# The order of copies and products in VectorE's queue, in a batched trace of matrix products

## The chip, the cores and the metric

One core of a Trainium2 chip. The metric is the device time of a run in microseconds (us), median of several runs. The profile's span, from the first to the last instruction, is about 1.7 us shorter.

## The reference

```python
def setup_inputs():
    B, N = 8, 2176
    return {
        "a": np.random.randn(B, N, N).astype(np.float32),
        "b": np.random.randn(B, N, N).astype(np.float32),
    }

def reference(a, b):
    prod = np.matmul(a, b)
    traces = np.diagonal(prod, axis1=1, axis2=2).sum(axis=-1)
    return traces.astype(np.float32)
```

The trace of a product is the sum over all i, k of a[i, k] * b[k, i]. So no matrix product is needed: transpose A, multiply elementwise by B, add up. Every input byte is read once.

## The kernel before

For each of eight batches: A is loaded as bf16 (the load casts) in two loads of 8 row tiles (4352 KB each) and one of a single row tile (544 KB). TensorE transposes A into PSUM tiles, of which there are five. ScalarE copies two of three of them to SBUF, VectorE the third. Then B is loaded in the same sizes and VectorE multiplies it by the transposed A, row tile by row tile, with a running sum. The large loads of A and B share three buffers, the single tiles two, and there is one buffer for the transposed A (`at`). In the last batch TensorE takes part of the products.

```python
    at_pool = ctx.enter_context(tc.tile_pool(name="at_pool", bufs=1))
    stage = ctx.enter_context(tc.tile_pool(name="stage", bufs=3))
    single = ctx.enter_context(tc.tile_pool(name="single", bufs=2))
    ...
    psum_pool = ctx.enter_context(tc.tile_pool(name="psum", bufs=5, space=bass.MemoryType.PSUM))
    # ... (cut)
    def evacuate(dst, src):
        nonlocal evacs
        if evacs % 3 == 2:
            nc.vector.tensor_copy(out=dst, in_=src)
        else:
            nc.scalar.copy(out=dst, in_=src)
        evacs += 1
    # ... (cut)
    for bi in range(BATCH):
        # ... loads of A; transpose_group() transposes and evacuates each group (cut)
        def on_dve(x, y):
            nonlocal cols
            multiply_reduce(x, y, acc[:, cols:cols + 1])
            cols += 1

        for start, m, count in joined(b_groups):
            # ... the last tile of the last batch (cut)
            groups, _ = load(b[bi], start, m, count)
            for start, m, b_t in groups:
                v0 = start // P
                for s in range(m):
                    row = b_t[:, s, :]
                    # ... the last batch's share for TensorE (cut)
                    on_dve(wide_at(at, v0 + s, 0, n_wide), wide(row, 0, n_wide))
                if not last:
                    on_dve(at[:, v0:v0 + m, split:], b_t[:, 0:m, split:])
```

The program is written in data-flow form; a scheduler fixes each engine's queue when the kernel is built. The order it chose had put the first product of a batch ahead of three copies of the same batch's transposed A, in batches 2 to 8.

## Time and profile before

| | before |
|---|---|
| time, median of 3 runs | 711.24 us (711.16 to 711.25) |
| span of the profiled run | 709.5 us |
| read from HBM | 303.04 MB |
| busy: VectorE, TensorE, ScalarE | 58%, 29%, 28% |

The prediction below shows the page, the chain, the waits and the timeline. Two more views are wanted. The first is the list of groups (columns: line, engine, operation, out<-in, shapes, count, then busy us and mean ns of one, then idle time before them and what ended it). It gives VectorE's copies and their sizes:

```profile
L109 DVE COPY at<-ps 128x1024 bf16<-128x1024 bf16 x64 | 78.4, 1224 | 171.3 <-PE ps L154 171.3
L109 DVE COPY at<-ps 128x512 bf16<-128x512 bf16 x32 | 13.5, 422 | 5.1 <-PE ps L175 4.8
L109 DVE COPY at<-ps 128x128 bf16<-128x128 bf16 x7 | 1.5, 221 | 2.6 <-PE ps L175 2.6
```

The second is the list of loads (tile, issuing queue, count, KB each, median us from issue to landing). One large load needs some 20.6 us by itself (an estimate: its 4.456 MB at the mean 216 GB/s of the trace); what is above that is time spent behind other loads:

```profile
t<-in_a_dram POOLq DMA_DIRECT2D x16, 4352.0 KB, 43.9
t<-in_b_dram POOLq DMA_DIRECT2D x15, 4352.0 KB, 51.7
```

### The profile page before, as it was taken

Reading aid. Unit: us, or ns where it says so; the run is one execution under the profiler, and the core shown is the slowest. Engines: PE = TensorE matmul, PEld = TensorE weight load, DVE = VectorE, ACT = ScalarE, POOL = GpSimd, SP = SyncE. Lnnn points to the kernel's source line nnn. Section 1 sums busy time; section 2 is a strip of 40 time slices with the busy share of each in tenths; the row PEclk is TensorE's granted clock in tenths of the full one; section 3 lists DMA queues with packets and bytes.
Section 4 is the critical chain, followed back from the end, with each engine's and each line's share of the span. In section 5 each row is a group of like instructions: output and inputs, shape, how many; then the busy total and the mean of one; then the engine's idle time right before and its main releaser. Section 6 shows DMA issues by size and latency. Waiting matters only on the chain.

```text
span 709.5 us, 3709 instructions
## 1 busy us (share of the span) xinstructions
PE 205.6 (29%) x1406; PEld 192.3 (27%) x1406; DVE 408.9 (58%) x449; ACT 197.3 (28%) x210; POOL 34.7 (5%) x60
## 2 busy tenths in 40 slices
PE   1442006410055100651005600056000660005637
PEld 0432006410055100551005500056000660004636
DVE  0222996129962299523995249942499325993257
ACT  2443005430064200652006610066000660006600
POOL 1000000000010000100001000000000000000000
PEclk9977556775577655776557765577555775557768
DMA  9999999999999999999999999999999999999997
GB/s 220 220 219 217 208 220 220 218 213 211 222 220 217 212 216 218 220 217 214 214 219 220 216 213 216 219 219 216 212 217 220 218 216 212 218 218 215 219 209 140
DMA packets 11620, 152.32 MB, mean 215 GB/s; under 512 B 850, under 2 KB 1106, under 8 KB 3282
## 3 DMA queue, kind: packets, MB, share of 16 engines
q0 software_dynamic: 11456, 150.97, 100.0%
q1 hardware_dynamic: 146, 1.11, 0.5%
q8 instruction: 11, 0.18, 0.1%
q14 instruction: 7, 0.06, 0.0%
HBM read 303.04 MB, written 0.00 MB: 427 GB/s over the span
## 4 chain that ended last, share of the span: by engine, by line
DMA 55%; DVE 34%; issue 7%; another core or an unknown queue 1%; ACT 1%; PE 1%; POOL 0%; DVEq 0%; POOLq 0%
DMA t<-in_b_dram 42%; DVE scratch L121 33%; DMA t<-in_a_dram 12%; DVE at L109 1%; ACT at L111 1%; PE ps L154 0%; DVE acc L121 0%; DVEq L121 0%; POOL identity masks.py:199 0%; PE ps L175 0%; POOL identity masks.py:197 0%; PE total L294 0%; DVE late L121 0%; DVE result L298 0%
## 5 line engine op out<-in xcount | busy, mean ns | idle before, releaser
L121 DVE CUSTOM_DVE_ANT_1 scratch<-at,t 128x2048 bf16<-128x2048 bf16 (+1 forms) x156 | 310.5, 1990 | 112.9 <-DMA t<-in_b_dram 106.4
L111 ACT COPY at<-ps 128x1024 bf16<-128x1024 bf16 x208 | 194.9, 1046 | 485.4 <-PE ps L154 485.4
L154 PE MATMUL ps<-identity,t 128*128 128x128 f32 x1071 | 178.4, 333 | 496.8 <-DMA t<-in_a_dram 291.5
L154 PEld LDWEIGHTS ps<-identity,t 128*128 128x128 f32 x1071 | 164.8, 213 | 506.6 <-issue 283.9
L109 DVE COPY at<-ps 128x1024 bf16<-128x1024 bf16 (+2 forms) x104 | 92.8, 902 | 179.0 <-PE ps L154 171.3
L74 POOL DMA_DIRECT2D t<-in_a_dram x23 | 15.3, 668 | 365.6 <-DVE acc L121 224.6
L74 POOL DMA_DIRECT2D t<-in_b_dram x26 | 16.7, 642 | 288.6 <-PE ps L175 151.9
L175 PE MATMUL ps<-identity,t 128*128 128x128 bf16 x170 | 17.0, 224 | 2.3 <-DVE at L109 1.8
L279 PEld LDWEIGHTS <-at 128*128 128x128 bf16 x153 | 16.9, 117 | 2.2 <-issue 2.1
L279 PE MATMUL trace_ps<-t,at 128*128 128x128 bf16 x144 | 16.2, 288 | 1.4 <-DMA t<-in_b_dram 1.4
L175 PEld LDWEIGHTS <-t 128*128 128x128 bf16 x170 | 13.4, 102 | 4.6 <-issue 4.2
L121 DVE DVE_READ_ACCUMULATOR2_ANT acc<- 128x1 f32 x163 | 13.3, 82 | 0.0
L86 DVE CAST t<-words 128x1088 bf16<-128x1088 f32 x1 | 0.7, 727 | 4.9 <-DMA words<-in_a_dram 4.9
L121 DVE CUSTOM_DVE_ANT_0 scratch<-at,t 128x128 bf16<-128x128 bf16 x7 | 2.0, 291 | 0.2
L85 ACT CAST t<-words 128x1088 bf16<-128x1088 f32 x1 | 1.1, 1098 | 3.8 <-DMA words<-in_a_dram 3.8
L243 POOL DMA_DIRECT2D b_t<-in_b_dram x3 | 1.6, 537 | 7.4 <-PE trace_ps L279 7.4
L121 DVE CUSTOM_DVE_ANT_1 scratch<-at,b_t 128x256 bf16<-128x256 bf16 (+1 forms) x3 | 1.5, 510 | 0.1
L271 DVE TENSOR_REDUCE sums<-acc 128x1 f32<-128x22 f32 (+1 forms) x8 | 1.4, 175 | 0.3
L279 PE MATMUL trace_ps<-b_t,at 128*128 128x128 bf16 x9 | 1.4, 291 | 0.4 <-DMA b_t<-in_b_dram 0.4
L85 ACT ACT_TABLE_LOAD x1 | 1.3, 1283 | 0.7 <-PEq L317 0.7
L294 PE MATMUL total<-late,ones 128*1 128x1 f32 x8 | 0.8, 164 | 0.8 <-DVE late L121 0.8
L294 PEld LDWEIGHTS total<-late,ones 128*1 128x1 f32 x8 | 0.3, 80 | 1.2 <-DVE late L121 1.2
(14 smaller groups left out, 2.7 us busy)
## 6 DMA issues: line engine op xcount, KB each, us to landing
t<-in_a_dram POOLq DMA_DIRECT2D x16, 4352.0 KB, 43.9
t<-in_b_dram POOLq DMA_DIRECT2D x15, 4352.0 KB, 51.7
t<-in_b_dram POOLq DMA_DIRECT2D x9, 544.0 KB, 54.6
t<-in_a_dram POOLq DMA_DIRECT2D x7, 544.0 KB, 44.2
t<-in_b_dram POOLq DMA_DIRECT2D x1, 2176.0 KB, 43.6
words<-in_a_dram SPq DMA_DIRECT2D x1, 1088.0 KB, 5.0
t<-in_b_dram POOLq DMA_DIRECT2D x1, 1088.0 KB, 28.8
b_t<-in_b_dram POOLq DMA_DIRECT2D x1, 256.0 KB, 8.9
```

The lines of the kernel that those rows point to most:

```text
L74: issued = nc.gpsimd.dma_start(out=part, in_=rows)
L85: nc.scalar.copy(out=t[:, 0, :half], in_=plain[:, :half])
L86: nc.vector.tensor_copy(out=t[:, 0, half:], in_=plain[:, half:])
L109: nc.vector.tensor_copy(out=dst, in_=src)
L111: nc.scalar.copy(out=dst, in_=src)
L121: nc.vector.tensor_tensor_reduce(out=out, in0=x, in1=y, scale=1.0, scalar=0.0, op0=MUL, op1=ADD, accum_out=acc,)
L154: nc.tensor.transpose(ps[:, n * m + r, :], words[:, r, c0:c0 + step * (P - 1) + 1:step], tiles[f32],)
L175: last_transpose = nc.tensor.transpose(ps16[:, n, r, :], a_t[:, r, c0:c0 + P], tiles[bf16],)
L243: nc.gpsimd.dma_start(out=row[:, lo:hi], in_=b[bi, start:start + P, lo:hi])
L271: nc.vector.reduce_sum(out=tiles["sums"][:, bi:bi + 1], in_=acc[:, :cols], axis=mybir.AxisListType.X)
L279: nc.tensor.matmul(trace_ps, x, y, start=(n == 0), stop=(n == len(pe_work) - 1),)
L294: nc.tensor.matmul(total[:, BATCH - 1:BATCH], tiles["ones"], part, start=(n == 0), stop=(n == len(parts) - 1),)
```

## The change

Its intent is to keep VectorE from standing at a product whose B has not landed while copies with data ready, which TensorE needs done, stand behind it. An ordering edge, without a semaphore, goes from each product to the last VectorE copy of its batch.

```diff
     evacs = 0
+    last_copy = None
 
     def evacuate(dst, src):
-        nonlocal evacs
+        nonlocal evacs, last_copy
         if evacs % 3 == 2:
-            nc.vector.tensor_copy(out=dst, in_=src)
+            last_copy = nc.vector.tensor_copy(out=dst, in_=src)
         else:
             nc.scalar.copy(out=dst, in_=src)
         evacs += 1
@@
+
+        copies_end = last_copy
         acc = acc_pool.tile([P, 2 * NT], f32, tag="acc")
         cols = 0
 
         def on_dve(x, y):
             nonlocal cols
-            multiply_reduce(x, y, acc[:, cols:cols + 1])
+            with tc.issue_after(copies_end.ins):
+                multiply_reduce(x, y, acc[:, cols:cols + 1])
             cols += 1
```

## The prediction

> **What bounds the kernel now.** I read the page first (busy shares, the slices, the queues, the chain), then the chain in order of time, the waits, the timeline of one batch, and the windows of the last microseconds. From the page:
>
> ```profile
> span 709.5 us, 3709 instructions
> PE 205.6 (29%) x1406; PEld 192.3 (27%) x1406; DVE 408.9 (58%) x449; ACT 197.3 (28%) x210; POOL 34.7 (5%) x60
> ...
> DMA  9999999999999999999999999999999999999997
> GB/s 220 220 219 217 208 220 220 218 213 211 222 220 217 212 216 218 220 217 214 214 219 220 216 213 216 219 219 216 212 217 220 218 216 212 218 218 215 219 209 140
> ...
> HBM read 303.04 MB, written 0.00 MB: 427 GB/s over the span
> ...
> DMA 55%; DVE 34%; issue 7%; another core or an unknown queue 1%; ACT 1%; PE 1%; POOL 0%; DVEq 0%; POOLq 0%
> ```
>
> No compute engine is over 58%. The DMA row is 9 in every slice but the last, and the rate row is flat at 208 to 222 GB/s (counted as bf16, half of what is read), from the first slice to the last but one. So the transfers never pause. The last line, the shares of the chain, seems to say otherwise: a third of the end's path runs through VectorE. The chain in order of time shows why:
>
> ```profile
> 198.33 45.16 DMA t<-in_b_dram
> 243.54 0.08 issue
> 243.62 2.29 DVE scratch L121
> 245.92 1.47 DVE at L109 x2
> 247.39 2.20 DVE scratch L121
> 249.59 0.15 DVE at L109
> ...
> 285.81 45.08 DMA t<-in_b_dram
> ```
>
> This is one turn of a loop: B's first load lands (243.5), VectorE multiplies both large loads of B, which frees the buffer, the next batch's first B load is issued (285.81) and lands 45 us later. The period is 285.81 - 198.33 = 87.5 us, 42.3 of VectorE and 45.2 of transfer. But a large load is 4352 KB, and at the mean 216 GB/s it needs 4.456 MB / 0.216 = 20.6 us. The other 24.6 us of its 45.2 are the loads queued ahead of it. They are slack: if VectorE ends earlier, the load is issued earlier and queues longer. A batch moves 2 x 17 tiles of 544 KB, 18.9 MB, which at 216.5 GB/s is 87.5 us: exactly the period. The loop turns at the transfers' rate.
>
> The defect that the change aims at is in the waits and the timeline:
>
> ```profile
> DVE scratch L121 <- DMA t<-in_b_dram: 106.4, 10, 13.7
> PE ps L154 <- DVE at L109: 103.2, 17, 14.6
> ```
> ```profile
> 243.62 2.29 DVE L121 CUSTOM_DVE_ANT_1 scratch<-at,t 128x2048 bf16<-128x2048 bf16 x1 [13.63 <-DMA t<-in_b_dram]
> 245.84 0.08 DVE L121 DVE_READ_ACCUMULATOR2_ANT acc<- 128x1 f32 x1
> 245.84 1.55 DVE L109 COPY at<-ps 128x1024 bf16<-128x1024 bf16 x2
> 247.11 0.73 PEld L154 LDWEIGHTS ps<-identity,t 128*128 128x128 f32 x4 [14.80 <-DVE at L109]
> ```
>
> VectorE stands 13.6 us at a product whose B has not landed, with three copies queued behind it. TensorE can't go on, because those copies hold PSUM tiles (there are five), and waits 14.6 us for the first of them. Both waits occur once per batch in batches 2 to 8; 7 x 14 us is most of both totals above.
>
> **What the Trainium skill says.** "Perfetto Trace Analysis", section "Per-engine timelines": ACT, DVE and GPSIMD are strict FIFO. The trace agrees: copies whose PSUM data was ready did not pass the waiting product. "DMA: Bandwidth & Descriptors", sections "Specifications" and "Measured": the fabric ceiling of a core is 435 GB/s, 425 were measured for a 16 MB load. The trace agrees: 427 GB/s over the span, and 2 x 216.5 = 433 in steady state, within 1% of the ceiling. "Perfetto Trace Analysis", "Identifying Performance Opportunities": improve the most-contended engine. Here that is the DMA engines, which this change gives no less work.
>
> **The change part by part.** It adds no instruction and removes none. It puts an ordering edge from each product of a batch to that batch's last VectorE copy, so the queue order on VectorE alone changes.
>
> 1. Batch 1: its lone row tile of A comes first, and the last copy already stands at 57.71 us, before the first product at 68.74. Nothing moves.
>
> 2. Batches 2 to 8: three copies (1224, 422 and 221 ns by the groups' rows) go ahead of the first product. TensorE filled the banks until about 232.5 us in the batch shown; the five copies and transposes left (three on VectorE, two on ScalarE at 1047 ns) then end near 235. B lands at 243.5, so the copies lie in idle time, with about 8 us to spare.
>
> 3. After B lands, VectorE has 1.87 us of copies less; they overlapped a little. The stretch from first product to the end of the first large B load is 177.79 - 156.14 = 21.65 us in batch 2, with copies, and 89.05 - 68.74 = 20.31 in batch 1, without. So VectorE gains about 1.3 us per batch. (A wait for the second B load, which lands 20.6 us after the first, may eat part.) The two A loads released by the first half and the B load released by the second are issued 1 to 1.5 us earlier. On the path this is nothing: the shortest time to landing of a large load in steady state is 42 us (issue at 178.09, landing 220.3) for 20.6 us of own transfer, so 21 us are queued ahead. The backlog grows to 22 to 23.
>
> 4. The last batch: its lone row of A releases the buffer of the last but one B tile. Its transposes, now at 686.2 behind the blocked copies, should run near 673, so that load goes out near 673 in place of 687.0. TensorE's products of B, queued behind those transposes (first at 686.49), start when B lands, near 682. The last B tile, now issued at 694.9, waits for the buffer of the first B load: TensorE's 72 products at 111 ns would end near 690, VectorE's four at 2.33 us near 691.3; it goes out near 691.5, 3.4 us earlier.
>
> Does that move the end? Windows of the last stretch (columns: PE, PEld, DVE, ACT, POOL busy, clock, DMA share, GB/s):
>
> ```profile
> 694.00:695.00 1.00, 1.00 (x12) 1.00 (x11) 1.00 (x1) 0.00 (x0) 0.10 (x1) 1.00 1.02 213
> ...
> 699.00:700.00 1.00, 0.11 (x2) 0.11 (x2) 0.00 (x0) 0.00 (x0) 0.00 (x0) 1.00 1.05 210
> ...
> 703.00:704.00 1.00, 1.00 (x12) 1.00 (x10) 0.97 (x3) 0.00 (x0) 0.00 (x0) 0.50 0.56 101
> 704.00:705.00 1.00, 0.80 (x7) 0.56 (x6) 0.96 (x4) 0.00 (x0) 0.00 (x0) 0.50 0.14 24
> ```
>
> The DMA share stays near 1 until 703. The last pieces, issued at 694.9 with 7.7 us queued ahead of 1.2 us of own transfer, came at line rate. Issued at 691.5 they would land at the same time. The last VectorE stretch begins at 700.00, when the two-row load lands at 699.85 (issued at 671.04, when the transposes of A's second large load are done, which does not change), and it runs without a gap to the end at 707.5. Before it VectorE stood idle for 2.4 us; that becomes about 3 to 4. TensorE had 0.4 us of waits left there and keeps up.
>
> Sum: 0 per batch on the path, 0 at the end. 711.24 less a few tenths at most.
>
> **The rivals.** (a) VectorE's share of the chain is real, and each turn gets shorter: 7 x 1.3 = 9 us, 702 us (1.3% faster). For it: the chain. Against: the flat rate, and 21 us of backlog. (b) The wait changes its name: products wait for the last copy in place of B. It would cost if the copy came after B. Against: A's lone row is issued before B in the same queue, so lands some 20 us earlier, and about 8 us are spare; only if the new order also delayed A's loads would a few us per batch be lost, 715 to 725. (c) The tail reorders. One single-row product (1.27 us) may move into VectorE's idle stretch before 700, which would end about 0.9 us earlier (limited by the last piece, which came at about 705.2): 710.3. Or TensorE, idle longer before 700, is slower: 0 to 1 us more, 712. Its matmuls there took 0.11 us at clock 0.5 as at 1.0, which speaks against it.
>
> **Range and chances.** I predict 711.1 us. 709.8 to 712.4 should hold it 8 times in 10: it covers (c) on both sides and a chip's own scatter. Faster by over 2% means under 697.0 us. The reads alone need 303.04 MB / 435 GB/s = 696.6 us by the skill's ceiling (an estimate), and start and tail add about 7: 0.01. Slower by over 2% (725.5) needs (b) at its worst: 0.02. Within 2%: 0.97.
>
> **What would show it right or wrong.** Right: the waits of TensorE for VectorE's copies fall from 103 us to a few; every large load's time to landing grows by 1 to 2 us; the rate row stays as it is; VectorE's busy time is unchanged and its wait for B stays near 100 us; the last B tile is issued near 691.5 but lands at about the same time. Wrong: slices of the rate row that rise by over 1% (then the DMA did have gaps), a period other than 87.5 us, products that wait for copies after B has landed, or large loads issued in another order.

## The result and the profile after

| | before | after |
|---|---|---|
| time, median of 6 runs each | 711.25 us (711.16 to 711.62) | 711.14 us (710.94 to 711.24) |
| span of the profiled run | 709.5 us | 709.4 us |

The ratio is 0.9997, 95% interval 0.9984 to 1.001. A ratio here is the mean time of one kernel's fast runs over the mean of the other's fast runs of the same rounds, so it is not quite the ratio of the medians in the table. The time is the same.

From the page of the kernel after, the rates of the 40 slices (share of the DMA engines, and GB/s counted as bf16):

```profile
DMA  9999999999999999999999999999999999999996
GB/s 220 220 220 219 206 219 220 219 217 209 219 220 218 217 212 216 220 219 215 212 218 220 218 213 215 215 222 217 215 214 213 225 217 212 215 217 222 219 207 138
```

The transfers look as before. In the trace's records of single packets there is no moment without one in flight between 1.8 us and the last data, at 704.9 us before and 704.8 after.

The waits of the kernel after (who, for whom, us in total, times, longest; its line numbers are one higher than before):

```profile
DVE at L110 <- PE ps L155: 196.9, 64, 19.9
DVE scratch L122 <- DMA t<-in_b_dram: 67.7, 17, 10.4
PE ps L155 <- DVE at L110: 2.7, 8, 0.4
```

TensorE's wait for VectorE's copies fell from 103.2 us to 2.7. The change does what it was made for. But TensorE's idle time before transposes, whatever it is put down to, fell only from 496.8 to 482.5 us: by the profile's account most of that wait has been traded for waits for the next batch's A and for the end of a batch's products. VectorE's wait for B fell from 106.4 to 67.7 us and its wait for TensorE grew by 26 us: the same idle time, cut differently, because copies now lie in the middle of it. The timeline of the third batch shows them there:

```profile
231.22 1.22 DVE L110 COPY at<-ps 128x1024 bf16<-128x1024 bf16 x1 [0.83 <-PE ps L155]
...
232.92 0.42 DVE L110 COPY at<-ps 128x512 bf16<-128x512 bf16 x1 [0.47 <-PE ps L176]
233.18 0.70 POOL L74 DMA_DIRECT2D t<-in_a_dram  x1 [20.62 <-PE ps L176]
...
234.24 0.22 DVE L110 COPY at<-ps 128x128 bf16<-128x128 bf16 x1 [0.89 <-PE ps L176]
234.50 0.56 POOL L74 DMA_DIRECT2D t<-in_a_dram  x1 [0.63 <-PE ps L176]
243.52 2.29 DVE L122 CUSTOM_DVE_ANT_1 scratch<-at,t 128x2048 bf16<-128x2048 bf16 x1 [9.05 <-DMA t<-in_b_dram]
```

The three copies end at 234.46, and VectorE is idle for 9.05 us until B lands. The two lines of POOL show a thing that the prediction did not foresee: from the fourth batch on, A's single tile (the shorter issue at 234.50) is now issued ahead of A's second large load. Before, it came behind it. The transposes that release its buffer now end earlier; that the scheduler moved it for this reason is likely, but no run shows it.

Where the 1.3 us went is seen in the chain of the kernel after (start us, us, what), against 45.16 and 45.08 for the same loads before:

```profile
197.15 46.24 DMA t<-in_b_dram
...
243.52 2.29 DVE scratch L122
245.85 2.29 DVE scratch L122
...
284.54 46.25 DMA t<-in_b_dram
```

The products of the first large B load, from the start of the first to the last reading of an accumulator, took 263.82 - 243.52 = 20.30 us, against 265.28 - 243.62 = 21.66 before: 1.36 us less. The next B load was issued at 284.54, 1.27 us earlier than before (285.81). It took 1.17 us longer to land. All but 0.1 us was given back in the queue, and that 0.1 us is older than the change's effect: already the first batch's first load of B landed 0.08 us earlier (68.52 against 68.60). From there to the end every large load lands 0.07 to 0.11 us earlier than before, but for A's second ones from the fourth batch on, which the single tile now precedes.

The tail (columns as in the prediction: five engines' busy us, clock, DMA share, GB/s) is the same too:

```profile
694.00:695.00 1.00, 1.00 (x12) 1.00 (x10) 0.97 (x3) 0.00 (x0) 0.00 (x0) 0.50 1.04 218
699.00:700.00 1.00, 0.21 (x3) 0.20 (x3) 0.09 (x1) 0.00 (x0) 0.00 (x0) 0.50 1.05 209
703.00:704.00 1.00, 1.00 (x12) 1.00 (x10) 0.96 (x3) 0.00 (x0) 0.00 (x0) 0.55 0.53 96
```

The last B tile was issued at 691.92, 3 us earlier than before, and its last piece landed at 705.07, against 705.16.

### The profile page after: what moved, and what is told of

Same layout as the page of the kernel before. It is cut to its first block, busy times and chain, and to the rows that moved or that the text cites. A ratio compares the mean times of both kernels' runs of the same rounds, so it can differ in the third digit from the quotient of the medians.

```text
span 709.4 us, 3709 instructions
## 1 busy us (share of the span) xinstructions
PE 206.3 (29%) x1406; PEld 193.0 (27%) x1406; DVE 411.4 (58%) x449; ACT 196.8 (28%) x210; POOL 34.6 (5%) x60
## 2 busy tenths in 40 slices
DMA packets 11620, 152.32 MB, mean 215 GB/s; under 512 B 850, under 2 KB 1106, under 8 KB 3282
## 3 DMA queue, kind: packets, MB, share of 16 engines
HBM read 303.04 MB, written 0.00 MB: 427 GB/s over the span
## 4 chain that ended last, share of the span: by engine, by line
DMA 56%; DVE 34%; issue 7%; PE 2%; another core or an unknown queue 2%; POOL 0%; DVEq 0%; POOLq 0%
DMA t<-in_b_dram 43%; DVE scratch L122 33%; DMA t<-in_a_dram 13%; PE ps L155 1%; DVE acc L122 0%; DVEq L122 0%; PE ps L176 0%; POOL identity masks.py:199 0%; DVE at L110 0%; POOL identity masks.py:197 0%; PE total L298 0%; DVE result L302 0%; DVE late L122 0%; POOLq L74 0%
## 5 line engine op out<-in xcount | busy, mean ns | idle before, releaser
L122 DVE CUSTOM_DVE_ANT_1 scratch<-at,t 128x2048 bf16<-128x2048 bf16 (+1 forms) x156 | 310.6, 1991 | 74.9 <-DMA t<-in_b_dram 67.7
L155 PE MATMUL ps<-identity,t 128*128 128x128 f32 x1071 | 177.9, 334 | 482.5 <-DVE sums L275 262.7
```

The costliest lines, as they stand in the source:

```text
L122: nc.vector.tensor_tensor_reduce(out=out, in0=x, in1=y, scale=1.0, scalar=0.0, op0=MUL, op1=ADD, accum_out=acc,)
L155: nc.tensor.transpose(ps[:, n * m + r, :], words[:, r, c0:c0 + step * (P - 1) + 1:step], tiles[f32],)
```

## The experiments

The theory: the transfers alone set the time; VectorE's part of the chain is hidden by loads that are queued ahead, so what the change saves only lengthens the queue. The rival: VectorE's third of the chain is real, and about 9 us were gained and lost again elsewhere. A third reading, that the old order cost VectorE nothing in the first place, is told apart by the last pair below.

### The loads by themselves

All transposes, copies and products are taken out; each load is followed by one VectorE copy of one column, so that buffers are reused as before. Its output is wrong, which doesn't matter for the time.

```diff
+    for bi in range(BATCH):
+        last = bi == BATCH - 1
+        for start, m, count in joined(a_groups):
+            touch(load(a[bi], start, m, count)[0])
+        for start, m, count in joined(row_groups(P, fine if last else even)):
+            touch(load(b[bi], start, m, count)[0])
```

> The kernel's loads with its buffers, each followed by one tiny VectorE copy; no transposes, no products; the result is wrong on purpose. Theory (the transfers alone set the time, the change moves nothing on the path): 703 to 709 us, that is the 711.2 of both kernels less 2 to 8 us of start and tail. Rival (VectorE's third of the chain is real, and the change's 9 us were lost elsewhere): well below 700 us, 620 to 690, because the loads would run ahead of what VectorE lets them do.

Measured: 710.38 us (709.84 to 711.43), before on the same chip 711.26, ratio 0.999 (0.9975 to 1.0004). Its rates:

```profile
GB/s 173 220 220 215 210 219 220 220 211 212 221 220 220 211 211 222 220 218 209 217 220 220 218 209 218 220 219 215 212 218 220 219 212 214 219 220 219 212 213 142
```

This is over the 703 to 709 expected: it starts its first load 1.4 us later than the kernel does, and its last tile waits for a buffer and lands at 706.55. From first to last data it takes 706.26 - 3.17 = 703.1 us; the kernel before takes 704.89 - 1.76 = 703.1. Some of that is a lull of its own making: the last tile landed 4.8 us after the one before it, where 2.6 would do, so without the lull it would be some 701 us (an estimate). Taking away all the arithmetic takes 0 to 2 us off the transfers. The rival, 620 to 690 us, is out.

### Half of the products

The kernel before, each long product cut to half its width. Its output is wrong, which doesn't matter for the time.

```diff
             nonlocal cols
+            if len(x.shape) == 3 and x.shape[2] == n_wide * P:
+                x, y = x[:, 0:2, :], y[:, 0:2, :]
             multiply_reduce(x, y, acc[:, cols:cols + 1])
```

> The kernel before with each long product cut to half its width (1024 of 2048 elements); wrong on purpose. VectorE's stretch of a batch, 42 us for two large loads of B, falls to about 24. Theory: 708 to 711 us (only the tail after the last large load gets shorter, by 1 to 2 us). Rival, VectorE on the path: 7 x 18 us less, about 585 us, or any fall of more than 10 us.

Measured: 710.58 us (710.42 to 710.66) against 711.26, ratio 0.999 (0.9975 to 1.0005). VectorE's busy time fell by 132 us, from 408.9 to 276.9, and the time by 0.7. In the profile the last instructions end that much earlier, the last data at the same 704.9.

### More products: how much VectorE work is hidden

The kernel after, with 4, 8 or 12 more products per batch in batches 1 to 7, written to a column that nobody adds. The results are right.

```diff
                 multiply_reduce(x, y, acc[:, cols:cols + 1])
+                if not last and cols in (0, 1, 2, 3):
+                    for _ in range(3):      # 1 and 2 in extra4 and extra8
+                        multiply_reduce(x, y, acc[:, 2 * NT - 1:2 * NT])
```

> The changed kernel with four more products of 2.33 us in each of batches 1 to 7 (into a column of the accumulator that nobody reads; the result stays right): 9.3 us more VectorE work per batch, seven times what the change takes off its path. Theory: the loads queued ahead (about 25 us) hide it: 710.5 to 712.5 us. Rival, VectorE on the path: 711 + 7 x 9.3 = 776 us.

> The changed kernel with eight more products per batch, 18.7 us. By extra12 (28 us more gave 50 us, 7.2 per batch) the slack is about 28 - 7.2 = 20.8 us, so 18.7 is still hidden: 711 to 713 us. If the slack is under 18 us: 7 us or more on top.

> Twelve more products per batch, 28 us. Theory with its size: after the changed kernel's trace the slack of a turn is 13 us (between the first and second large load of A) plus 6 to 9 us (between the last copy and the landing of B), about 19 to 22 us; what is over it comes on the path: 711 + 7 x (28 - 20) = 767, 750 to 785 us. Rival, VectorE on the path throughout: 711 + 7 x 28 = 907 us. If the slack were over 28 us: 711.

| | more VectorE work per batch | time, us | before, same chip | ratio (95%) |
|---|---|---|---|---|
| extra4 | 9.3 us | 711.06 | 711.26 | 0.9997 (0.998 to 1.0013) |
| extra8 | 18.7 us | 711.41 | 711.24 | 1.0002 (0.9988 to 1.0016) |
| extra12 | 28.0 us | 761.75 | 711.26 | 1.0708 (1.068 to 1.0736) |

Fourteen times what the change saves per batch can be added without a trace in the time. Then the slack is used up. The step from extra8 to extra12 is 50 us, 7.2 per batch, so by this the slack is about 28 - 7.2 = 20.8 us of VectorE work per batch (an estimate that takes each us past the limit at full cost). The rates of extra8, and of extra12 in its second run below, show the two sides of the limit:

```profile
GB/s 220 220 219 212 212 220 219 214 218 212 221 218 214 219 215 217 219 215 218 215 217 219 215 216 217 213 222 217 214 217 212 223 218 213 218 214 221 218 208 136
```

```profile
GB/s 219 220 220 209 216 207 161 211 213 218 194 162 209 217 218 193 176 204 217 215 185 186 204 217 215 176 190 198 215 214 180 191 198 218 216 176 176 205 209 145
```

In extra8 the row is as flat as in both kernels, though VectorE is busy 76% of the time. In extra12 it dips once per batch, to 161 to 185 at the lowest: the queue of loads runs dry, and only then does VectorE's time show.

### The old order where VectorE is on the path

The same twelve products per batch, added to the kernel before (old order) and, again, to the kernel after, on one chip. If the old order really costs VectorE time, it must show here. Both kernels have A's single tile ahead of A's second load, so the order of loads doesn't tell them apart.

```diff
 # extra12_oldorder: the kernel before, with the added lines and no ordering edge
-            with tc.issue_after(copies_end.ins):
-                multiply_reduce(x, y, acc[:, cols:cols + 1])
+            multiply_reduce(x, y, acc[:, cols:cols + 1])
```

> The kernel before (old order on VectorE) with the twelve more products per batch. In extra12 the loads queue ran dry and VectorE's work after the landing of B came onto the path (a turn took 94.9 us: 48.7 of products, then two transfers). There the copies that the old order puts behind the first product must cost what I said they take, about 1.3 us per batch: 7 x 1.3 = 9 us over extra12, 767 to 774 us. Rival (the change takes nothing off VectorE, or only moves it elsewhere): the same as extra12, 759 to 764.

> extra12 once more, on the same chip as extra12_oldorder: 759 to 764 us.

Measured: old order 769.99 us (768.73 to 771.4, ratio to before 1.0825, 1.0811 to 1.084), new order 761.88 us (760.32 to 763.39, ratio 1.0711, 1.0696 to 1.0725). The intervals are apart. The difference is 8.1 us, 1.16 per batch; 9 was expected. The timelines show what it consists of. New order, then old order, third batch:

```profile
256.59 0.23 DVE L110 COPY at<-ps 128x128 bf16<-128x128 bf16 x1 [0.89 <-PE ps L176]
...
257.56 2.29 DVE L122 CUSTOM_DVE_ANT_1 scratch<-at,t 128x2048 bf16<-128x2048 bf16 x1 [0.75 <-DMA t<-in_b_dram]
...
306.17 0.70 POOL L74 DMA_DIRECT2D t<-in_a_dram  x1 [48.76 <-DVE acc L122]
```
```profile
258.58 2.29 DVE L121 CUSTOM_DVE_ANT_1 scratch<-at,t 128x2048 bf16<-128x2048 bf16 x1 [5.68 <-DMA t<-in_b_dram]
...
260.80 1.55 DVE L109 COPY at<-ps 128x1024 bf16<-128x1024 bf16 x2
...
264.48 0.22 DVE L109 COPY at<-ps 128x128 bf16<-128x128 bf16 x1
...
308.54 0.70 POOL L74 DMA_DIRECT2D t<-in_a_dram  x1 [44.37 <-DVE acc L121]
```

In the new order the copies have ended when B lands (VectorE is idle for 0.75 us between them and the first product), and the buffer of B's first load is free 48.61 us after the first product began (306.17 - 257.56). In the old order it takes 49.96 (308.54 - 258.58), with the three copies inside; the next two batches read the same. That is 1.35 us per batch, the same as in the kernels themselves. So the old order does cost VectorE 1.3 us per batch, the change does remove it, and in the tuned kernel nobody is waiting for it. The third reading is out.

### Two load buffers in place of three

If it is the queued loads that hide VectorE, taking one buffer away must bring VectorE's work onto the path at a dose that three buffers hide.

```diff
-    stage = ctx.enter_context(tc.tile_pool(name="stage", bufs=3))
+    stage = ctx.enter_context(tc.tile_pool(name="stage", bufs=2))
```

> The changed kernel with two large load buffers in place of three, so that at most about one load is queued ahead. Theory: the backlog falls from 25 us to nearly 0, and the time rises a little, by the moments in which a buffer comes free late: 712 to 735 us. If no backlog were needed: 711.

> bufs2_after with the four more products of extra4, 9.3 us of VectorE work per batch, which three buffers should hide or have hidden. Theory (it is the queued loads that hide VectorE, not idle time on VectorE): most of 7 x 9.3 = 65 us appears, 740 to 790 us. Rival (VectorE's idle time hides it whatever the buffers): within 3 us of bufs2_after.

Measured: 714.14 us (713.65 to 714.37), ratio 1.0034 (1.0018 to 1.0051); with four more products per batch 777.97 us (777.3 to 778.77), ratio 1.0934 (1.0918 to 1.0951); before on the same chip 711.55. Three buffers hid 9.3 us per batch wholly (extra4); two let 63.8 us through, 9.1 per batch. The median time to landing of a large load tells of the queue. In the kernel after, then with two buffers:

```profile
t<-in_a_dram POOLq DMA_DIRECT2D x16, 4352.0 KB, 46.7
t<-in_b_dram POOLq DMA_DIRECT2D x15, 4352.0 KB, 51.5
```
```profile
t<-in_a_dram POOLq DMA_DIRECT2D x16, 4352.0 KB, 25.6
t<-in_b_dram POOLq DMA_DIRECT2D x15, 4352.0 KB, 30.0
```

Against 20.6 us of own transfer, some 26 to 31 us of queue have become 5 to 9. With two buffers the kernel itself is hardly slower: the loads just keep up, with almost nothing to spare. The pair that was wanted first, old against new order with two buffers, could not be had so simply: with two buffers the scheduler puts the copies first by itself, so both sources give the same VectorE order (seen by building both; the old source with two buffers was not run).

### A version aimed at the tail

The last stretch on VectorE runs without a gap from the landing of the two-row load at 699.75. One product in it belongs to a tile that landed at 694.6. It can be taken in the idle time before.

```diff
+        b_loads = joined(b_groups)
+        if last:
+            b_loads[2], b_loads[3] = b_loads[3], b_loads[2]
-        for start, m, count in joined(b_groups):
+        for start, m, count in b_loads:
```

> The changed kernel, but in the last batch the single-row tile of B that has landed at 694.6 is multiplied before the two-row load that lands at 699.75, in VectorE's 3 us of idle time. That takes one product of 1.27 us out of the last stretch; the last piece lands at 705.07 whatever VectorE does, so about 0.9 us: 710.2 us, 709.9 to 710.6. If TensorE's order or the loads' order shifts too: no gain.

Measured: 710.48 us (710.13 to 710.85, 5 runs), against 711.24 (710.93 to 711.8) for before, ratio 0.9989 (0.9975 to 1.0002). The product did move (a 128x1024 product at 697.03 in place of 702.24), and VectorE's last copy came at 706.59 in place of 707.24. The gain seen, 0.8 us against before on the same chip, is of the size expected, but the interval includes 1: likely, not shown. No faster version with a right result was found. What is left after its last data (704.99 us in the trace) is 5.5 us of the 710.48, 1.8 of them outside the span.

## Why the prediction was right

The time (711.1 predicted, 711.14 measured) and the class came out, and by the steps given:

- The bound. The loads alone take 703.1 us of transfer, as in the kernel, of which a lull of 2 us is their own. Right.
- Step 1, batch 1 unmoved. Its first product was to stay at 68.74; it began at 68.66, right after the first B load (landed at 68.60 before, 68.52 after). Right.
- Step 2, the copies fit into idle time. In the third batch they ended at 234.46 (near 235 predicted), 9 us before B (8 predicted). Right, but the spare time is smaller from the fourth batch on, 6.3 to 6.8 us, where A's second large load lands 2.5 us later than before. It was still enough.
- Step 3, 1.3 us per batch off VectorE, and nothing of it on the path. 1.36 us in the kernel's third batch, 1.35 and 1.16 per batch in the pair with twelve more products; the next B load took 1.1 to 1.2 us longer to land. Right in sign and size, and here not only argued: 1.16 us per batch do show in the time once the slack is gone.
- Step 4, the last batch. TensorE's products of B began at 681.80 (near 682), the last tile was issued at 691.92 (near 691.5) and landed 0.1 us earlier. The single-row load before it went out at 675.36 in place of 687.00 (near 673 predicted). Right. One step in it failed: the two-row load's issue "does not change". It went from 671.04 to 674.06, because A's second large load landed 2.5 us later (661.13 in place of 658.62), with the single tile now ahead of it. It still landed at 699.75, behind what was queued.
- The rivals. Wait (b) did not come: no product waited for a copy with B landed. Tail (c) did not happen by itself, and made by hand it gave about what was said (0.8 us of 0.9), though within the noise.

Two of the signs to look for were wrong, and a third by a little. "Every large load's time to landing grows by 1 to 2 us": only that of loads released by VectorE did, 1.1 us for B's first load, and 3.9 for A's second (42.2 to 46.1 in the fourth batch), most of which is the single tile of 2.6 us that moved ahead of it. A's first load, released by TensorE, took less: 53.95 in place of 54.96 in the fourth batch and 2.7 to 3.7 us less in the later ones, being issued later by nearly as much. B's second load, also released by TensorE, changed by 0.7 us at most, either way. "VectorE's wait for B stays near 100 us": it fell to 67.7, because the copies now cut the idle time in two, and the first part counts as a wait for TensorE. "VectorE's busy time is unchanged": it rose from 408.9 to 411.4 us; before, the records of the moved copies overlapped those of the products beside them. And loads in another order were named as a sign against; they came, in the one place told above, and cost nothing, since a reordered queue moves the same bytes.

## What to carry to other kernels

An engine's share of the chain that ended last is not yet time to be gained: where the chain runs through a load, compare the load's time to landing with its own transfer time, and what is above that is slack which swallows any gain ahead of it, and a loss up to its own size (here some 21 us). If the transfers are never idle and near their rate, an order of instructions can only matter at the start and in the tail. A dose of added work (here 4, 8 and 12 products) measures the slack, and a kernel in which the slack is used up shows whether a "useless" change was well aimed.

## What the Trainium skill lacked or had wrong

- "DMA: Bandwidth & Descriptors", sections "Specifications" and "Measured": the page has no figure for casting loads. A stream of loads that cast from float32 to bf16 reads 427 GB/s over a whole 709 us span and 433 (2 x 216.5, about the mean of the rate row without its last slice) in steady state, close to the page's ceiling of 435 GB/s and its 425 measured for 16 MB. But the page puts that ceiling at the ports of SBUF, and only half of the bytes read is written there (152.32 MB of packets for 303.04 MB read); no run shows which part sets the rate of casting loads.
- "Perfetto Trace Analysis", section "Identifying Dependency Chains": it says how to follow waits, but not that a load's time to landing has queueing in it. Here 24 to 26 of 45 to 46 us were queue, and VectorE's apparent 34% of the chain was worth nothing: 132 us less VectorE work took 0.7 us off.
- "TensorE: Matmul & The Clock Gate", section "Back-to-back issue gap": for a stream of pairs of weight load and matmul it gives about 81 ns per matmul at 128 columns. In the last batch, where each matmul has a weight load before it, they came 0.11 to 0.12 us apart at a granted clock of 0.5 and of 1.0 alike (median 0.116 in both). Why was not looked into.
